# Layer norm with a tile of its own for the centred, weighted row: one step out of place instead of in place

## The chip, the cores and the metric

The kernel runs on one core of a Trainium2 chip. The metric is the device time of one execution in microseconds (us); the median of three executions of the kernel before is 1938.56 us (1937.89 to 1939.11). The core's engines run their own instruction streams in order and meet through semaphores: TensorE (PE in the profile, with PEld for its weight loads), VectorE (DVE), ScalarE (ACT), GpSimd (POOL) and SyncE (SP), which issues most DMAs.

## The reference

Two decoder layers over x of 512 tokens by 1024 channels in float32. Each layer is a half-step SwiGLU FFN, a token mixer (layer 0: differential attention; layer 1: causal pooling), cross-attention into 256 memory tokens, and a second FFN. Every one of these eight sublayers ends in a layer norm over the 1024 channels of the residual sum:

```python
def layer_norm(x, g, b):
    xf = x.astype(jnp.float32)
    mu = jnp.mean(xf, axis=-1, keepdims=True)
    var = jnp.mean(jnp.square(xf - mu), axis=-1, keepdims=True)
    y = (xf - mu) * lax.rsqrt(var + LN_EPS) * g.astype(jnp.float32) + b.astype(jnp.float32)
    return y.astype(x.dtype)
...
    for i in range(DEPTH):
        x = layer_norm(a * x + 0.5 * swiglu_ffn(x, ffn_w_in[i, 0], ffn_w_out[i, 0]), ln_g[i, 0], ln_b[i, 0])
        ...  # h = diff_attention(x, ...) in layer 0, pool_mixer(x, ...) in layer 1
        x = layer_norm(a * x + h, ln_g[i, 1], ln_b[i, 1])
        x = layer_norm(a * x + memory_cross_attention(x, mem, xa_wq[i], xa_wkv[i], xa_wo[i]), ln_g[i, 2], ln_b[i, 2])
        x = layer_norm(a * x + 0.5 * swiglu_ffn(x, ffn_w_in[i, 1], ffn_w_out[i, 1]), ln_g[i, 3], ln_b[i, 3])
```

## The kernel before

The 512 tokens are four tiles X[0] to X[3] of 128 tokens by 1024 channels, kept in SBUF as float32 for the whole run. Every product is made of three matmuls of split operands: a value is split into a high part (ScalarE's cast, L114) and a low part (VectorE's subtraction, L115), and `mm3` (L201 to L203) runs high by high, high by low and low by high. So nearly everything that TensorE reads, weights (wh, wl) and activations (xh, xl), passes through ScalarE and VectorE first.

A sublayer's last product gives 128x512 blocks `ps` in PSUM, in the order LAST: (half, token tile) = (0,0), (0,1), (1,0), (1,1), (0,2), (1,2), (0,3), (1,3). `ln_add` (L397, VectorE) adds each block into X and collects its row sums. When the second half of a token tile is in, `ln_token` runs for it; there are 8 norms of 4 token tiles, 32 in all. Its steps:

- L406, VectorE: the (negative) mean from the two row sums.
- L419, ScalarE ("square"): Square of X plus the mean, summed along the row into `var`. The squares themselves go to a throw-away bfloat16 tile `sq`, taken from the buffers of the tag `self.spare`: sp in the FFNs, rt in differential attention, p in cross-attention, sq in the pooling mixer.
- L420 and L421, GpSimd: variance times 1/D plus epsilon, and its power -0.5, both on 128x1 values.
- L423, VectorE ("begin"): (X plus mean) times g, written to y. In the kernel before y is X itself, so this write comes after ScalarE's read of X. The one exception is the last token tile of the last norm, where y is two tiles of the tag sp.
- L425, VectorE ("end"): y times the power of L421 plus b, written to X.

The gain g and the shift b are loaded by DMA into tiles of the phase's tags (`self.gain`): hr and sr in the FFNs, v and v in differential attention, gb and gb in cross-attention, pooled and pooled in the pooling mixer (there as two halves each, and begin and end go in two 128x512 instructions; so they do in the last norm).

After end, TensorE transposes X (L479, `turn`) into `pt`, and ScalarE and VectorE split the transposes into xh and xl, the next sublayer's operands. `turn_late` puts these transposes behind given matmuls (`issue_after`), so their place in TensorE's stream is set by hand. `split_weights` puts some weight splits behind a norm's square and end (gates, L241 and L243). `queue_behind` in `ffn` puts the last token tile's square and begin behind the first weight split of the next FFN.

The order within each engine's stream comes from a planner that takes instructions by their place in the program and by its own estimate of when their inputs are ready, and that gives a tile a buffer of its tag when one has been released. A buffer is released when all instructions that use the tile are done. Each phase (FFN, mixer, cross-attention) opens its own pools over the same memory, so that a buffer of the next phase waits for the tile that had the place before.

In cross-attention, `xa_head` holds the softmax rows of two token tiles in one p tile (128x2x256), two such tiles for a head, out of 4 buffers; `turn_memory` loads the 256 memory tokens into 4 tiles of the same tag before the first head.

Of the kernel before, what the change touches and what calls it, by code (L numbers as in the profile page):

```python
# [17 lines left out]
P = 128  # L18
D = 1024
S = 512  # L20
# [5 lines left out]
MEM = 256  # L26
# [73 lines left out]
def drain(units):  # L100
    for _ in units:
        pass


class Trunk:
# [40 lines left out]
        self.pad(ctx, APART)  # L146

    @contextmanager
    def phase_pool(self, gain, spare, **bufs):

        self.gain, self.spare, self.bufs, self.phase = gain, spare, bufs, {}
        with ExitStack() as ctx:
            for t in bufs:
                if t == "_x":
                    self.to_x(ctx)
                else:
                    self.phase[t] = ctx.enter_context(self.pool(t))
            yield  # L160
# [240 lines left out]
    def ln_token(self, t):  # L401
        nc, X = self.nc, self.X[t]
        g, b = self.ln_gb
        s = self.ln_sums[t]
        mean, var, rstd = (self.small(n, (P, 1)) for n in ("mean", "var", "rstd"))
        nc.vector.tensor_scalar(mean, s[:, 0:1], s[:, 1:2], -1.0 / D, ALU.add, ALU.mult)  # L406
        if self.last_ln or not self.wide_gain:
            cols = [slice(half * S, (half + 1) * S) for half in range(2)]
        else:
            cols = [slice(0, D)]  # L410
        if self.wide_gain:
            g, b = ([x[0][:, c] for c in cols] for x in (g, b))
        y = [X[:, c] for c in cols]
        if self.last_ln and t == NT - 1:
            y = [self.tmp(self.spare) for _ in range(2)]
            sq = self.act(self.gain[0], (P, D), mybir.dt.bfloat16)
        else:
            sq = self.act(self.spare, (P, D), mybir.dt.bfloat16)
        square = nc.scalar.activation(sq, X, AF.Square, bias=mean, accum_out=var)  # L419
        nc.gpsimd.tensor_scalar(var, var, 1.0 / D, EPS * self.ln_scale**2, ALU.mult, ALU.add)  # L420
        nc.gpsimd.tensor_tensor(rstd, var, self.mhalf[:, 0:1], ALU.pow)  # L421
        for i, c in enumerate(cols):
            begin = nc.vector.scalar_tensor_tensor(y[i], X[:, c], mean, g[i], ALU.add, ALU.mult)  # L423
        for i, c in enumerate(cols):
            end = nc.vector.scalar_tensor_tensor(X[:, c], y[i], rstd, b[i], ALU.mult, ALU.add)  # L425
            if self.last_ln:
                nc.sync.dma_start(self.out[t * P : (t + 1) * P, c], X[:, c])
        self.ends.append((square, end))
        self.begins = square, begin
        if t == NT - 1:  # L430
            self.gates = list(self.next_gates)
        if self.make_xt:
            self.late.append(t)
# [794 lines left out]
    def turn_memory(self, tag):  # L1228

        nc = self.nc  # L1230
        src = self.a["mem"][0].rearrange("(m p) (h d) -> p m h d", p=P, h=2)
        raw = [[self.tmp(tag) for h in range(2)] for m in range(2)]
        for m in range(2):
            for h in range(2):
                nc.sync.dma_start(raw[m][h], src[:, m, h])
        self.memT = []
        for c in range(0, KC, 2):
            pt = self.aux("pt").rearrange("p (c m n) -> p c m n", c=2, m=2)
            for i in range(2):
                for m in range(2):  # L1240
                    o = (c + i) % 4 * P
                    self.nc.tensor.transpose(pt[:, i, m], raw[m][c // 4][:, o : o + P], self.ident)
            t = self.mem_tile(c)
            self.split(t[:, 0], t[:, 1], pt.rearrange("p c m n -> p c (m n)"))
        self.stage["mem"].tile([P, (480 - LINE) // 4], F32, name="mempad")
# [47 lines left out]
    def xa_head(self, qs, kt, v):  # L1293
        nc = self.nc
        pT = [self.pair("pT") for _ in range(2)]
        ps = []
        for tt in range(0, NT, 2):
            sc = self.aux("xs").rearrange("p (t n) -> p t n", t=2)
            for i in range(2):
                o = slice((tt + i) * P, (tt + i + 1) * P)  # L1300
                for c in range(2):
                    q = qs[c]
                    self.mm3(
                        sc[:, i], (q[0][:, o], q[1][:, o]), (kt[0][:, c], kt[1][:, c]), c == 0, c == 1
                    )
            mx, sm, rc = self.small("mx"), self.small("sm"), self.small("rx")
            nc.vector.tensor_reduce(mx, sc, AX.X, ALU.max, negate=True)
            p = self.tmp("p", (P, 2, MEM))
            for i in range(2):
                nc.scalar.activation(  # L1310
                    p[:, i], sc[:, i], AF.Exp, bias=mx[:, i : i + 1], accum_out=sm[:, i : i + 1]
                )
            nc.vector.reciprocal(rc, sm)
            for i in range(2):
                nc.vector.tensor_scalar(p[:, i], p[:, i], rc[:, i : i + 1], None, ALU.mult)
            ps.append(p)
            yield
        for tt in range(0, NT, 2):
            p = ps[tt // 2]
            pt = self.aux("pt").rearrange("p (m i n) -> p m i n", m=2, i=2)  # L1320
            for m in range(2):
                for i in range(2):
                    nc.tensor.transpose(pt[:, m, i], p[:, i, m * P : (m + 1) * P], self.ident)
            for m in range(2):
                o = slice(tt * P, (tt + 2) * P)
                self.split(pT[m][0][:, o], pT[m][1][:, o], pt[:, m].rearrange("p i n -> p (i n)"))
            yield
        for c in range(2):
            e = slice(c * P, (c + 1) * P)
            po = self.aux("xo")  # L1330
            for m in range(2):
                self.mm3(po, (v[0][:, m, e], v[1][:, m, e]), pT[m], m == 0, m == 1)
            o = self.pair("oT")
            self.split(o[0], o[1], po)
            self.oT.append(o)
            yield
# [45 lines left out]
    def cross_attention(self, layer, ln):  # L1382
        bufs = dict(q=8, oT=10, gb=2)
        if layer == 0:
            self.kv = []
            mem = self.side_pool("mem")
            with self.other_pools():
                self.stage["mem"] = mem
                with self.phase_pool(("gb", "gb"), "p", pT=6, p=4, kv=8, _x=0, **bufs):
                    self.kvp = self.phase["kv"]  # L1390
                    self.mem_tiles = []
                    with self.tc.high_priority():
                        self.turn_memory("p")
                    self.xa(layer, ln)
            self.close_side()
        else:
            with self.later, self.phase_pool(("gb", "gb"), "p", pT=6, p=4, **bufs):
                self.xa(layer, ln)

    def xa(self, layer, ln):  # L1400
# [58 lines left out]

    def ffn_phase(self, **more):  # L1460
        bufs = dict(b1=1, b3=1, b2=1, b4=1, _x=0, xe=6, hb=4, sp=4, ha=4, sr=1, hr=3)
        return self.phase_pool(("hr", "sr"), "sp", **bufs, **more)

    def ffn_first(self, layer, ln):
        with self.ffn_pools():
# [13 lines left out]
    def mixer(self, layer, ln):  # L1479
        if layer == 0:  # L1480
            bufs = dict(low=4, rt=2, a=4, p=4, o=1, qk=8, _x=0, v=4, oT=11, mask=1)
            with self.other_pools(), self.phase_pool(("v", "v"), "rt", **bufs):
                self.diff_attention(layer, ln)
            self.close_side()
        else:
            w = self.a["xa_wkv"][layer]
            self.later = ExitStack()
            self.later.enter_context(self.late_pools())
            self.kvp = self.later.enter_context(self.pool("kv"))
            with self.phase_pool(("pooled", "pooled"), "sq", pooled=20, sq=1):  # L1490
                with self.tc.high_priority():
                    keys = self.load_cols(w, 0, "rawe")
                    self.load_memory()
                    ahead = [self.halves(t, "we", "we") for t in keys]
                    self.pool_weights()
                    self.raw_order = ["rawe", "raw", "raw"]
                side = self.pool_mixer(layer, ln)
                next(side)
                self.kv = []
                self.weave(self.first_heads(layer, ahead), side, 900, 6000)  # L1500
                drain(self.early_kv(layer, (1,), self.ahead))
            self.close_side()
# [40 lines left out]
```

## Time and profile before

| what | value |
|---|---|
| median of three executions | 1938.56 us (1937.89 to 1939.11) |
| profiled execution: its own time, its span | 1939.3 us, 1937.5 us |
| granted TensorE clock | 0.999 |
| PE busy | 1904.6 us (98%) |
| DVE busy | 1555.8 us (80%) |
| ACT busy | 1015.8 us (52%) |
| POOL busy | 334.8 us (17%) |

The span runs from the first to the last instruction; 1.8 us of the profiled execution's own time lie around it. A row of the timeline gives the start and the duration in us, then engine, line, operation, names (out<-in) and shapes, and in brackets the idle time of the engine before it and what ended that. Rows of equal instructions right behind each other are merged (x2, x4). A row of the waits gives the total, the number and the longest. Engine queues have a q (SPq issues DMAs). A line can be a helper's: L114 and L115 are all splits.

### The profile page before, as it was taken

The page shows a single profiled execution, that of the slowest core. Times are in us where ns is not written, and L with a number is a line of the kernel's source. Part 1 is how long each engine was busy: PE and PEld are TensorE (multiplying, and loading weights), DVE is VectorE, ACT ScalarE, POOL GpSimd, SP SyncE. Part 2 cuts the span into 40 slices and gives each one's busy share as a digit, 9 for nine tenths or more (in the row PEclk, how much of TensorE's full clock was granted, in tenths as well). Part 3 has the DMA queues.
Part 4 walks back from the last instruction along what each step waited for, and adds up shares of the span by engine and source line. Part 5 has one row for each costly group of instructions (what it writes and reads, how often), then busy time and mean ns, then how long its engine had stood idle before and what let it go on. Part 6 is the DMA issues. An engine that isn't in the chain of part 4 may idle for free.

```text
span 1937.5 us, 32405 instructions
## 1 busy us (share of the span) xinstructions
PE 1904.6 (98%) x12988; PEld 1738.8 (90%) x12988; DVE 1555.8 (80%) x2262; ACT 1015.8 (52%) x1543; POOL 334.8 (17%) x318
## 2 busy tenths in 40 slices
PE   9999999999999999999999999999999999999998
PEld 8999998888888888999998999999898889999996
DVE  7988887888867558788888988898886568898886
ACT  6655553567755435645554655455454436555552
POOL 2212121111211002211220321212110013211211
PEclk9999999999999999999999999999999999999999
DMA  9878772322126326978784688877444337777861
GB/s 253 198 173 185 171 145 66 92 67 87 56 97 196 109 66 153 218 175 163 141 193 135 114 203 174 178 161 164 142 153 141 109 87 122 190 174 168 187 140 44
DMA packets 254199, 280.46 MB, mean 145 GB/s; under 512 B 9184, under 2 KB 221792, under 8 KB 254048
## 3 DMA queue, kind: packets, MB, share of 16 engines
q0 software_dynamic: 95808, 102.77, 32.6%
q1 hardware_dynamic: 158240, 175.61, 28.6%
q8 instruction: 102, 1.67, 0.3%
q14 instruction: 49, 0.40, 0.1%
HBM read 274.15 MB, written 4.20 MB: 144 GB/s over the span
## 4 chain that ended last, share of the span: by engine, by line
PE 70%; DVE 17%; ACT 4%; DMA 4%; issue 2%; POOL 2%; SPq 0%; DVEq 0%; POOLq 0%; ACTq 0%
PE x L202 6%; PE x L201 6%; PE x L203 6%; PE z L202 4%; PE z L201 4%; PE z L203 4%; DVE wl L115 4%; PE ps L203 3%; PE ps L202 3%; DMA ra<-in_ffn_w_in_dram 3%; PE ps L201 3%; PE px L201 2%; PE px L203 2%; PE px L202 2%; PE xq L202 2%
## 5 line engine op out<-in xcount | busy, mean ns | idle before, releaser
L636 POOL DMA_DIRECT2D ra<-in_ffn_w_in_dram x132 | 170.4, 1315 | 988.3 <-DVE wl L115 971.4
L114 ACT CAST wh<-ra 128x1024 fp32r<-128x1024 f32 x184 | 193.3, 1053 | 209.1 <-PE x L202 56.0
L115 DVE TENSOR_TENSOR wl<-ra,wh 128x1024 fp32r<-128x1024 f32 x184 | 224.0, 1223 | 68.0 <-ACT wh L114 67.2
L114 ACT CAST wh<-rc 128x1024 fp32r<-128x1024 f32 x136 | 142.8, 1052 | 117.7 <-PE x L202 42.5
L201 PE MATMUL x<-xe,wh 128*128 128x256 f32 x704 | 195.6, 278 | 1.6 <-ACT sp L697 1.6
L201 PE MATMUL x<-xh,wh 128*128 128x256 f32 x704 | 196.0, 278 | 0.7 <-ACT xh L114 0.7
L202 PE MATMUL x<-xl,wh 128*128 128x256 f32 x704 | 195.6, 278 | 0.3 <-DVE xl L115 0.3
L203 PE MATMUL x<-xh,wl 128*128 128x256 f32 x704 | 195.6, 278 | 0.4 <-DVE wl L115 0.4
L202 PE MATMUL x<-xe,wh 128*128 128x256 f32 x704 | 195.3, 277 | 0.0
L203 PE MATMUL x<-xe,wl 128*128 128x256 f32 x704 | 195.3, 277 | 0.0
L114 ACT CAST wh<-b 128x1024 fp32r<-128x1024 f32 x112 | 117.8, 1051 | 128.6 <-PE x L202 63.2
L115 DVE TENSOR_TENSOR wl<-rc,wh 128x1024 fp32r<-128x1024 f32 x136 | 164.9, 1222 | 23.2 <-ACT wh L114 23.2
L115 DVE TENSOR_TENSOR wl<-b,wh 128x1024 fp32r<-128x1024 f32 x112 | 137.0, 1224 | 41.1 <-ACT wh L114 41.1
L201 PEld LDWEIGHTS x<-xe,wh 128*128 128x128 f32 x704 | 132.5, 188 | 3.2 <-ACT sp L697 1.8
L202 PEld LDWEIGHTS x<-xl,wh 128*128 128x128 f32 x704 | 132.7, 188 | 2.1 <-DVE xl L115 0.8
L201 PEld LDWEIGHTS x<-xh,wh 128*128 128x128 f32 x704 | 132.3, 188 | 2.2 <-ACT xh L114 0.9
L202 PEld LDWEIGHTS x<-xe,wh 128*128 128x128 f32 x704 | 132.5, 188 | 1.4
L203 PEld LDWEIGHTS x<-xh,wl 128*128 128x128 f32 x704 | 132.3, 188 | 0.6 <-DVE wl L115 0.6
L203 PEld LDWEIGHTS x<-xe,wl 128*128 128x128 f32 x704 | 132.4, 188 | 0.0
L203 PE MATMUL y<-xh,wl 128*128 128x256 f32 x352 | 98.8, 281 | 2.1 <-DVE wl L115 1.2
L201 PE MATMUL y<-xh,wh 128*128 128x256 f32 x352 | 98.1, 279 | 0.2 <-ACT wh L114 0.2
L202 PE MATMUL z<-xe,wh 128*128 128x256 f32 x352 | 97.8, 278 | 0.3 <-DVE xe L115 0.3
(401 smaller groups left out, 6056.0 us busy)
## 6 DMA issues: line engine op xcount, KB each, us to landing
ra<-in_ffn_w_in_dram POOLq DMA_DIRECT2D x132, 512.0 KB, 6.9
rc<-in_ffn_w_in_dram SPq DMA_DIRECT2D x88, 512.0 KB, 6.1
b<-in_ffn_w_out_dram SPq DMA_DIRECT2D x60, 512.0 KB, 5.0
ra<-in_ffn_w_in_dram SPq DMA_DIRECT2D x44, 512.0 KB, 5.0
rc<-in_ffn_w_in_dram POOLq DMA_DIRECT2D x44, 512.0 KB, 7.2
b<-in_ffn_w_out_dram POOLq DMA_DIRECT2D x16, 512.0 KB, 12.6
raw<-in_da_w_qkv_dram SPq DMA_DIRECT2D x16, 512.0 KB, 5.1
raw<-in_xa_wkv_dram SPq DMA_DIRECT2D x8, 1024.0 KB, 5.5
```

The lines of the kernel that those rows point to most:

```text
L114: self.nc.scalar.copy(hi, src),
L115: self.nc.vector.tensor_sub(lo, src, hi.bitcast(F32)),
L201: mm(out, w[0], x[0], start=start, stop=False, skip_group_check=again)
L202: mm(out, w[0], x[1], start=False, stop=False, skip_group_check=again)
L203: self.last_mm = mm(out, w[1], x[0], start=False, stop=stop, skip_group_check=again)
L636: self.last_more = nc.gpsimd.dma_start(t, source(*block), accum_op=ALU.add)
```

## The change

Begin writes y to a tile of its own (`home`): a whole 128x1024 tile, or two 128x512 tiles in the pooling mixer. The tag of this tile is a new argument of `phase_pool`: hr in the FFNs, v in differential attention, p in cross-attention, pooled in the pooling mixer. The last token tile of the last norm stays as it was. To have buffers of 128x1024 under the tag p, `xa_head` and `turn_memory` take p tiles of double size, and p has 2 buffers in place of 4, so the same bytes; pooled has 22 buffers in place of 20; hr (3) and v (4) keep theirs.

```diff
     @contextmanager
-    def phase_pool(self, gain, spare, **bufs):
+    def phase_pool(self, gain, spare, home, **bufs):
-        self.gain, self.spare, self.bufs, self.phase = gain, spare, bufs, {}
+        self.gain, self.spare, self.home = gain, spare, home
+        self.bufs, self.phase = bufs, {}
...
         if self.wide_gain:
             g, b = ([x[0][:, c] for c in cols] for x in (g, b))
-        y = [X[:, c] for c in cols]
         if self.last_ln and t == NT - 1:
             y = [self.tmp(self.spare) for _ in range(2)]
             sq = self.act(self.gain[0], (P, D), mybir.dt.bfloat16)
         else:
             sq = self.act(self.spare, (P, D), mybir.dt.bfloat16)
+            if self.wide_gain:
+                whole = self.tmp(self.home, (P, D))
+                y = [whole[:, c] for c in cols]
+            else:
+                y = [self.tmp(self.home) for _ in cols]
...
     def turn_memory(self, tag):
-        raw = [[self.tmp(tag) for h in range(2)] for m in range(2)]
+        raw = [self.tmp(tag, (P, 2, S)) for m in range(2)]
         for m in range(2):
             for h in range(2):
-                nc.sync.dma_start(raw[m][h], src[:, m, h])
+                nc.sync.dma_start(raw[m][:, h], src[:, m, h])
...
-                    self.nc.tensor.transpose(pt[:, i, m], raw[m][c // 4][:, o : o + P], self.ident)
+                    self.nc.tensor.transpose(pt[:, i, m], raw[m][:, c // 4, o : o + P], self.ident)
...
     def xa_head(self, qs, kt, v):
-        ps = []
+        ps = self.tmp("p", (P, 2, 2, MEM))
         for tt in range(0, NT, 2):
...
-            p = self.tmp("p", (P, 2, MEM))
+            p = ps[:, tt // 2]
...
-            ps.append(p)
             yield
         for tt in range(0, NT, 2):
-            p = ps[tt // 2]
+            p = ps[:, tt // 2]
...
-                with self.phase_pool(("gb", "gb"), "p", pT=6, p=4, kv=8, _x=0, **bufs):
+                with self.phase_pool(("gb", "gb"), "p", "p", pT=6, p=2, kv=8, _x=0, **bufs):
...
-            with self.later, self.phase_pool(("gb", "gb"), "p", pT=6, p=4, **bufs):
+            with self.later, self.phase_pool(("gb", "gb"), "p", "p", pT=6, p=2, **bufs):
...
-        return self.phase_pool(("hr", "sr"), "sp", **bufs, **more)
+        return self.phase_pool(("hr", "sr"), "sp", "hr", **bufs, **more)
...
-            with self.other_pools(), self.phase_pool(("v", "v"), "rt", **bufs):
+            with self.other_pools(), self.phase_pool(("v", "v"), "rt", "v", **bufs):
...
-            with self.phase_pool(("pooled", "pooled"), "sq", pooled=20, sq=1):
+            with self.phase_pool(("pooled", "pooled"), "sq", "pooled", pooled=22, sq=1):
```

## The prediction

> **What bounds the kernel now.** I read the page first, then TensorE's waits, then a table of stretches, then the timeline around the norms.
>
> ```profile
> span 1937.5 us, 32405 instructions
> ...
> PE 1904.6 (98%) x12988; PEld 1738.8 (90%) x12988; DVE 1555.8 (80%) x2262; ACT 1015.8 (52%) x1543; POOL 334.8 (17%) x318
> ...
> PE 70%; DVE 17%; ACT 4%; DMA 4%; issue 2%; POOL 2%; SPq 0%; DVEq 0%; POOLq 0%; ACTq 0%
> ```
>
> TensorE's waits for the norm's end, for `ln_add`, and for VectorE where the memory is transposed:
>
> ```profile
> PE pt L479 <- DVE X L425: 4.2, 5, 2.5
> ```
>
> ```profile
> PE ps L201 <- DVE X L397: 1.3, 1, 1.3
> ```
>
> ```profile
> PE pt L1242 <- DVE xl L115: 1.2, 3, 0.5
> ```
>
> And the last stretch (length, then busy time of PE, PEld, DVE, ACT, POOL):
>
> ```profile
> 1929.70:1937.50 7.80, 0.00 (x0) 0.00 (x0) 3.59 (x7) 1.24 (x2) 0.73 (x2) 0.81 0.18 67
> ```
>
> TensorE is busy for 1904.6 of 1937.5 us, so 32.9 us are idle, and 7.8 us of those are the tail after its last matmul. A change to the norms can only be worth what TensorE waits for them. The three rows of waits say how little that is: 4.2 us in five waits of transposes (L479) for a norm's end (L425), one wait of 1.3 us for a PSUM buffer that `ln_add` (L397) frees late, and 1.2 us in three waits behind VectorE in the stage where the memory is transposed.
>
> **The norm's chain, before and after.** The first norm's last token tile, VectorE, then ScalarE, then GpSimd:
>
> ```profile
> 343.48 0.21 DVE L406 TENSOR_SCALAR mean<-sums 128x1 f32<-128x1 f32 x1
> 345.00 1.28 DVE L423 SCALAR_TENSOR_TENSOR X<-X,mean,hr 128x1024 f32<-128x1024 f32 x1 [1.31 <-ACT sp L419]
> ...
> 347.05 1.28 DVE L425 SCALAR_TENSOR_TENSOR X<-X,rstd,sr 128x1024 f32<-128x1024 f32 x1 [0.44 <-POOL rstd L421]
> ```
>
> ```profile
> 343.73 1.15 ACT L419 ACTIVATE sp<-X,mean 128x1024 bf16<-128x1024 f32 x1 [3.59 <-DVE mean L406]
> ```
>
> ```profile
> 345.06 1.28 POOL L420 TENSOR_SCALAR var<-var 128x1 f32<-128x1 f32 x1 [8.70 <-ACT sp L419]
> 346.42 0.59 POOL L421 TENSOR_TENSOR rstd<-var,mhalf 128x1 f32<-128x1 f32 x1
> ```
>
> Mean to end takes 347.05 - 343.48 = 3.57 us. VectorE idles 1.31 us until the square has read X. Then begin and GpSimd's L420 start together, and L420, a 128x1 instruction, takes as long as begin (1.28 us). The last norm's last token tile already has its y elsewhere:
>
> ```profile
> 1930.28 0.21 DVE L406 TENSOR_SCALAR mean<-sums 128x1 f32<-128x1 f32 x1
> 1930.53 1.41 DVE L423 SCALAR_TENSOR_TENSOR sp<-X,mean,hr 128x512 f32<-128x512 f32 x2
> 1930.61 1.15 ACT L419 ACTIVATE hr<-X,mean 128x1024 bf16<-128x1024 f32 x1 [7.02 <-DVE mean L406]
> ```
>
> ```profile
> 1931.94 0.19 POOL L420 TENSOR_SCALAR var<-var 128x1 f32<-128x1 f32 x1 [6.50 <-ACT hr L419]
> 1932.21 0.54 POOL L421 TENSOR_TENSOR rstd<-var,mhalf 128x1 f32<-128x1 f32 x1
> 1932.79 1.42 DVE L425 SCALAR_TENSOR_TENSOR X<-sp,rstd,sr 128x512 f32<-128x512 f32 x2 [0.84 <-POOL rstd L421]
> ```
>
> This is the changed form, measured: begin and square side by side at their usual length (the square 1.15 us in both), L420 in 0.19 us since begin is over, and mean to end 1932.79 - 1930.28 = 2.51 us. The change is worth 3.57 - 2.51 = 1.06 us of chain for a token tile where VectorE has nothing else to do. Part of it is the square, part is GpSimd no longer running beside begin.
>
> The Trainium skill, page "SBUF — State Buffer", section "Who interferes with whom", says that a VectorE instruction with two SBUF inputs and a GpSimd instruction that reads SBUF exclude each other for the whole instruction, and the later one waits. This trace agrees (1.28 us beside begin, 0.19 us alone). The rule also speaks against the change: any other such VectorE instruction behind begin holds GpSimd just as well, and if that happened at every token tile the sum below would fall to what the square alone gives, or less.
>
> **The change part by part.**
>
> Instructions: none is added or removed on any engine. 32 means, squares and pairs on GpSimd, and as many begins and ends, keep shape and length; writing to another tile costs nothing (1.41 us for two halves in the row above). VectorE is as busy as before; what changes is where it idles and the planner's order, since begin is ready right after the mean.
>
> The tail: the last token tile already has this form, and TensorE's end lies ahead of it. Worth 0.
>
> First norm, last token tile. TensorE's waits behind it, and what stands between:
>
> ```profile
> 348.39 1.09 PE L479 MATMUL pt<-ident,X 128*128 128x128 f32 x8 [0.19 <-DVE X L425]
> 350.22 0.38 PE L201 MATMUL v<-wh,xh 128*128 128x256 f32 x1 [0.74 <-ACT xh L114]
> 351.19 0.50 PE L201 MATMUL q<-xh,wh 128*128 128x512 f32 x1 [0.47 <-ACT xh L114]
> 352.31 0.39 PE L203 MATMUL v<-wh,xl 128*128 128x256 f32 x1 [0.62 <-DVE xl L115]
> ```
>
> ```profile
> 348.25 0.28 DVE L923 TENSOR_REDUCE lam_d<-p 128x2 f32<-128x128 f32 x1
> ```
>
> ```profile
> 348.20 1.28 ACT L924 ACT_TABLE_LOAD   x1
> 349.49 0.20 ACT L924 ACTIVATE lam_d<-lam_d 128x2 f32<-128x2 f32 x1
> 349.60 2.03 ACT L114 CAST xh<-pt 128x512 fp32r<-128x512 f32 x4
> ```
>
> The four waits are 0.19 + 0.74 + 0.47 + 0.62 = 2.02 us, all on one string: end, then L923 on VectorE, then L924 with its table on ScalarE, then the four casts xh, with VectorE's splits behind end as well. If the string starts 1.06 us earlier, TensorE gains that 1.06; the rest of the 2.02 stays. Bounds 0 (the planner puts another split ahead of end) and 2.02. I take 1.06.
>
> Norm of differential attention. Here three memory transposes wait behind VectorE; the first follows this:
>
> ```profile
> 580.79 1.28 DVE L425 SCALAR_TENSOR_TENSOR X<-X,rstd,v 128x1024 f32<-128x1024 f32 x1 [0.72 <-POOL rstd L421]
> ```
>
> ```profile
> 583.94 0.66 PE L1242 MATMUL pt<-ident,p 128*128 128x128 f32 x4 [0.53 <-DVE xl L115]
> ```
>
> End waited 0.72 us for GpSimd, and `ln_add` and the split xl stand behind it. With 1.06 us off, the 0.53 goes; what is late next are the two other memory transposes (1.2 - 0.53, about 0.6 us), behind VectorE's unbroken work. I take 0.53, between 0 and 1.2.
>
> Its last token tile is where GpSimd suffers most:
>
> ```profile
> 595.11 2.60 POOL L421 TENSOR_TENSOR rstd<-var,mhalf 128x1 f32<-128x1 f32 x1
> ```
>
> ```profile
> 599.18 1.06 PE L479 MATMUL pt<-ident,X 128*128 128x128 f32 x8 [0.62 <-DVE X L425]
> ```
>
> L421 takes 2.60 us against 0.54, a loss of 2.06 on the way to end, because VectorE runs weight splits and begin without a break. With begin earlier, a split still follows. TensorE's wait is 0.62; I take 0.40, between 0 and 0.62.
>
> Cross-attention of layer 0, first token tile:
>
> ```profile
> 741.12 1.23 DVE L115 TENSOR_TENSOR wl<-ra,wh 128x1024 fp32r<-128x1024 f32 x1 [0.84 <-ACT wh L114]
> 742.26 1.22 DVE L115 TENSOR_TENSOR wl<-rc,wh 128x1024 fp32r<-128x1024 f32 x1
> 743.40 1.28 DVE L423 SCALAR_TENSOR_TENSOR X<-X,mean,gb 128x1024 f32<-128x1024 f32 x1
> 744.59 0.68 DVE L397 SCALAR_TENSOR_TENSOR X<-X,ps 128x512 f32<-128x512 f32 x1
> ```
>
> Begin comes after two weight splits since its square is late, and `ln_add` behind it frees the PSUM buffer for which TensorE waits its 1.3 us. With begin ready at the mean, it fills the 0.84 us of idle time and the row of 744.59 comes 0.84 earlier. I take 0.84, between 0 and 1.3.
>
> The other waits of the group of 4.2: the longest, 2.54 us, is the pooling mixer's first token tile, whose begin waits for g itself:
>
> ```profile
> 1438.28 1.42 DVE L423 SCALAR_TENSOR_TENSOR X<-X,mean,pooled 128x512 f32<-128x512 f32 x2 [2.64 <-DMA pooled<-in_ln_g_dram]
> ```
>
> The change doesn't touch this load: 0. The two left are 4.2 - 2.54 - 0.19 - 0.62 = about 0.85 us in places where VectorE has no idle time; I take 0.20, between 0 and 0.85. The other norms' token tiles cost TensorE nothing now: their transposes stand far enough behind in its stream. If that cover went, the price is such a wait, at most the 1.3 us seen.
>
> Buffers. In cross-attention y and sq share the two p buffers: sq(t+1) takes the one that sq(t) left, y(t+1) the one that end(t) left, and end(t) is ahead of begin(t+1) on VectorE anyway: 0. A p tile of double size is released after the head's second half; heads run one after another, so the tile of two heads ago is free: 0. In hr and v the y's have free buffers beside the gains; pooled has two more. On SP, the four memory loads come in the same number and place; they are issued from 558.14 on:
>
> ```profile
> 558.14 2.69 SPq L1235 DMA_DIRECT2D p<-in_mem_dram  x4
> ```
>
> Their data are first read some 25 us later, at 583.94, so a wait for a larger buffer, even of some us, is hidden, and so is the weight load behind them on that queue. y keeps its buffer until end instead of until begin, so the next phase's tiles in that place may come some 1.3 us later; POOL's memset of `mask` and its SP load are such, and the scores that read them come tens of us later: 0, with a bound of 0.5 us of loss.
>
> Sum: 1.06 + 0.53 + 0.40 + 0.84 + 0.20 = 3.03 us. Against the profiled execution: span 1937.5 to 1934.5, own time 1939.3 (1.8 around the span) to 1936.3. That execution is 0.74 us above the median of the three, so the median goes from 1938.56 to 1935.5. What a measurement of this kernel tells from no change is about 0.2%, 3.9 us: the forecast lies inside it.
>
> **The rivals.**
>
> More goes. All the touched waits together are 2.02 + 1.2 + 0.62 + 1.3 + 0.85 = 6.0 us, so 1932.6. For it: VectorE's lost idle time (1.31 us before each such begin) also pulls ahead splits that later matmuls wait for. Against it: each string has a next link, as in the first norm, where only half goes. Past 3.9 us this counts as faster.
>
> Nothing comes of it: 1938.5, give or take 1. The planner, told that begin is ready, fills the idle time with begin and then leaves VectorE idle before end (0.84 us in the tail's row) with the same instructions behind it; TensorE's waits move and stay as long. Or y finds no free buffer and waits for the square after all, above all with p, which serves both. For it: only 6 us of 1937.5 are there to win.
>
> Slower: end stalls VectorE. The planner sets end early, believing GpSimd done, while a split holds GpSimd as at 595.11; `ln_add` behind end then frees PSUM late, at 1.3 us a time, the largest such wait seen. Six norms with transposes behind them, one such wait in each: 7.8 us less the 3.0 won, so 1943.3. It decides from three such waits on. Against it: today's end has the same GpSimd ahead of it at 32 places and only one wait of this kind is in the trace.
>
> **How the numbers follow.** Forecast (a gain of 1 to 3.9 us): 0.37. More goes: 0.34. Nothing comes of it: 0.15. Slower than by 0.2%: 0.14. So faster 0.34, within 0.2% 0.52, slower 0.14. The range goes from the whole of the touched waits (1932.6) to a part of the slower case, one or two new waits beyond the gain, 1940.9; about 0.08 is left out below and 0.11 above. The forecast's own range is 1934.7 to 1937.6.
>
> **What would show it.** Right: L423 no longer idles for L419 and starts within 0.1 us of the mean's end; L420 falls from 1.28 us towards 0.2; mean to end nears 2.5 us; the one wait of L201 on L397 shrinks from 1.3 to some 0.4; the four waits near 350 sum to about 1; the 2.5 us of the pooling mixer and the 7.8 us tail stay. Wrong: new TensorE waits on L397 or L425; L421 at 2 us and more in many places; VectorE's order changed so that a split which TensorE needs comes behind a begin; or a changed SP order that moves the loads of g, in which case the 2.54 us would move by as much either way.

## The result and the profile after

Side by side on one chip, 14 runs each, the changed kernel has a median of 1936.1 us (1933.4 to 1939.6) and the kernel before 1938.6 us (1936.5 to 1941.6): ratio 0.9984 [0.9977, 0.9991], that is 1.7 to 4.5 us less. A second comparison, beside the experiments, gave 0.9986 [0.9978, 0.9995]. The forecast was 1935.5 us.

The page of the profiled execution after (its own time 1937.6 us):

```profile
span 1935.8 us, 32409 instructions
...
PE 1906.2 (98%) x12988; PEld 1743.4 (90%) x12988; DVE 1556.6 (80%) x2262; ACT 1016.7 (53%) x1543; POOL 308.5 (16%) x318
```

TensorE idles 1935.8 - 1906.2 = 29.6 us instead of 32.9, 3.3 us less; its busy time is 1.6 us longer, for the most part because 3.41 us near 1438 us ran at half clock (shown below), so the span is only 1.7 us shorter. VectorE is as busy as before; GpSimd has lost 26 us. The groups of begin and of GpSimd's two steps say why, first in the kernel before, then in the changed one (count, busy us, mean ns, then idle time before them and its releaser; lines have moved: L397 is now L398, L419 to L421 are L424 to L426, L423 is L428, L425 is L430, L479 is L484, L201 to L203 are L202 to L204):

```profile
L423 DVE SCALAR_TENSOR_TENSOR X<-X,mean,hr 128x1024 f32<-128x1024 f32 (+1 forms) x18 | 19.7, 1106 | 15.2 <-ACT sp L419 15.2
...
L420 POOL TENSOR_SCALAR var<-var 128x1 f32<-128x1 f32 x32 | 31.1, 973 | 264.4 <-ACT sp L419 169.9 <-ACT sq L419 37.5 <-ACT p L419 25.3
L421 POOL TENSOR_TENSOR rstd<-var,mhalf 128x1 f32<-128x1 f32 x32 | 24.1, 752 | 2.7
```

```profile
L428 DVE SCALAR_TENSOR_TENSOR hr<-X,mean,hr 128x1024 f32<-128x1024 f32 (+1 forms) x18 | 19.7, 1106 | 0.4
...
L426 POOL TENSOR_TENSOR rstd<-var,mhalf 128x1 f32<-128x1 f32 x32 | 19.2, 598 | 2.7
L425 POOL TENSOR_SCALAR var<-var 128x1 f32<-128x1 f32 x32 | 10.2, 318 | 282.8 <-ACT sp L424 179.8 <-ACT sq L424 32.1 <-ACT rt L424 29.3
```

Begin of the FFNs' norms idled 15.2 us for the square and now idles 0.4; GpSimd's first step falls from a mean of 973 ns to 318, which is 20.9 of the 26 us. The first norm's last token tile, on VectorE, ScalarE and GpSimd:

```profile
344.08 0.21 DVE L407 TENSOR_SCALAR mean<-sums 128x1 f32<-128x1 f32 x1
344.32 1.28 DVE L428 SCALAR_TENSOR_TENSOR hr<-X,mean,hr 128x1024 f32<-128x1024 f32 x1
346.51 1.28 DVE L430 SCALAR_TENSOR_TENSOR X<-hr,rstd,sr 128x1024 f32<-128x1024 f32 x1 [0.90 <-POOL rstd L426]
```

```profile
344.32 1.15 ACT L424 ACTIVATE sp<-X,mean 128x1024 bf16<-128x1024 f32 x1 [3.02 <-DVE mean L407]
```

```profile
345.65 0.19 POOL L425 TENSOR_SCALAR var<-var 128x1 f32<-128x1 f32 x1 [9.23 <-ACT sp L424]
345.93 0.55 POOL L426 TENSOR_TENSOR rstd<-var,mhalf 128x1 f32<-128x1 f32 x1
```

Begin and square start in the same 10 ns; mean to end is 346.51 - 344.08 = 2.43 us instead of 3.57. Of the four waits of TensorE behind it (2.02 us) one is left:

```profile
351.51 0.39 PE L204 MATMUL v<-wh,xl 128*128 128x256 f32 x1 [0.93 <-DVE xl L115]
```

The waits that answer to the prediction's groups, from the table of TensorE's waits after (total, times, longest):

```profile
PE pt L484 <- DVE X L430: 4.9, 3, 2.7
...
PE x L203 <- DVE xl L115: 1.5, 1, 1.5
...
PE pt L1247 <- DVE xl L115: 0.7, 1, 0.7
```

The wait for `ln_add` (1.3 us) has gone, the memory's transposes wait 0.7 instead of 1.2 us, the transposes of X wait 4.9 instead of 4.2 us, and a wait of 1.5 us for a split xl is new.

Where the time went, stage by stage, is read from the start times of equally numbered matmuls. The table gives the us between two such starts in the traces of the two kernels and of a second run of each (both described below):

| matmuls (us in the trace before) | before | again | after | again | mean difference |
|---|---|---|---|---|---|
| 2450-2550, first norm (348-367) | 19.59 | 21.01 | 17.86 | 17.85 | -2.44 |
| 3750-3950, norm of diff. attention (580-613) | 32.77 | 33.78 | 33.13 | 33.36 | -0.03 |
| 4700-4800, cross-attention, layer 0 (737-758) | 20.47 | 20.11 | 20.65 | 21.08 | +0.57 |
| 7200-8200, first FFN of layer 1 (1091-1220) | 129.11 | 130.31 | 128.36 | 128.36 | -1.35 |
| 9700-9900, pooling mixer (1436-1467) | 30.83 | 29.88 | 32.77 | 32.45 | +2.26 |
| 10750-11300, last FFN (1615-1683) | 68.19 | 68.57 | 67.68 | 67.71 | -0.68 |

The six sum to -1.7 us; the spans of the four traces differ by 1.95 us in the mean. Stages ahead of the first touched norm differ by about 1 us between traces too, so only lines that repeat carry weight. Three gains stand against two losses that the prediction had as 0 and as a gain. The second and third line don't stand clear of chance: the kernel of the first experiment below, in which begin is in place, took 32.07 and 21.37 us there.

### The profile page after: what moved, and what is told of

It is laid out like the page before. It is cut to its first block, busy times and chain, and to the rows that moved or that the text cites. A ratio compares the mean times of both kernels' runs of the same rounds, so it can differ in the third digit from the quotient of the medians.

```text
span 1935.8 us, 32409 instructions
## 1 busy us (share of the span) xinstructions
PE 1906.2 (98%) x12988; PEld 1743.4 (90%) x12988; DVE 1556.6 (80%) x2262; ACT 1016.7 (53%) x1543; POOL 308.5 (16%) x318
## 4 chain that ended last, share of the span: by engine, by line
PE 75%; DVE 14%; DMA 4%; ACT 4%; issue 2%; POOL 1%; SPq 0%; DVEq 0%; POOLq 0%; ACTq 0%
PE x L202 6%; PE x L203 6%; PE x L204 6%; PE ps L204 4%; PE ps L203 4%; PE ps L202 4%; PE z L202 4%; PE z L204 4%; PE z L203 4%; DVE wl L115 3%; DMA ra<-in_ffn_w_in_dram 2%; PE px L202 2%; PE px L204 2%; PE px L203 2%; PE y L204 2%
## 5 line engine op out<-in xcount | busy, mean ns | idle before, releaser
L202 PE MATMUL x<-xh,wh 128*128 128x256 f32 x704 | 196.9, 280 | 1.4 <-ACT xh L114 1.4
L203 PE MATMUL x<-xl,wh 128*128 128x256 f32 x704 | 196.6, 279 | 1.5 <-DVE xl L115 1.5
L204 PE MATMUL x<-xh,wl 128*128 128x256 f32 x704 | 196.3, 279 | 0.0
L202 PE MATMUL x<-xe,wh 128*128 128x256 f32 x704 | 195.7, 278 | 0.4 <-ACT sp L702 0.4
L203 PE MATMUL x<-xe,wh 128*128 128x256 f32 x704 | 195.5, 278 | 0.0
L204 PE MATMUL x<-xe,wl 128*128 128x256 f32 x704 | 195.4, 278 | 0.0
L203 PEld LDWEIGHTS x<-xl,wh 128*128 128x128 f32 x704 | 133.6, 190 | 3.3 <-DVE xl L115 2.0
L202 PEld LDWEIGHTS x<-xh,wh 128*128 128x128 f32 x704 | 132.9, 189 | 2.9 <-ACT xh L114 1.6
L202 PEld LDWEIGHTS x<-xe,wh 128*128 128x128 f32 x704 | 132.3, 188 | 1.9 <-ACT sp L702 0.6
L203 PEld LDWEIGHTS x<-xe,wh 128*128 128x128 f32 x704 | 132.7, 188 | 1.3
L204 PEld LDWEIGHTS x<-xh,wl 128*128 128x128 f32 x704 | 133.2, 189 | 0.0
L204 PEld LDWEIGHTS x<-xe,wl 128*128 128x128 f32 x704 | 132.5, 188 | 0.0
L204 PE MATMUL y<-xh,wl 128*128 128x256 f32 x352 | 98.7, 280 | 0.9
L202 PE MATMUL y<-xh,wh 128*128 128x256 f32 x352 | 98.2, 279 | 0.4 <-ACT wh L114 0.4
L202 PE MATMUL z<-xe,wh 128*128 128x256 f32 x352 | 97.9, 278 | 0.0
```

The lines of the kernel that those rows point to most:

```text
L202: mm(out, w[0], x[0], start=start, stop=False, skip_group_check=again)
L203: mm(out, w[0], x[1], start=False, stop=False, skip_group_check=again)
L204: self.last_mm = mm(out, w[1], x[0], start=False, stop=stop, skip_group_check=again)
```

## The experiments

All ratios are to the kernel before, run beside them.

**The new buffers alone, begin in place.** First question: does the gain come from begin's freedom, or from the buffers and the order that they bring?

```diff
-                y = [self.tmp(self.home) for _ in cols]   # and the whole tile
+        y = [X[:, c] for c in cols]
```

> The changed kernel's buffers (p 2 of double size, pooled 22), but y is X again: begin is in place. Theory A (the gain is the shorter way from mean to end, because begin no longer waits for the square): time as before, 1938.6 within its noise of about 1.5 us; begin idles about 1.3 us for the square; GpSimd's first step takes 1.28 us beside begin; TensorE's waits near 350 us sum to about 2.0 and the 1.25 us wait for ln_add near 745 us is back. Theory B (the gain comes from the buffers and the order that they give): time as the changed kernel, 1936.1, with the waits near 350 at about 0.9.

1940.6 us, ratio 0.9995 [0.9986, 1.0005]: no gain. TensorE's four waits near 350 us sum to 2.27 us, and it waits for `ln_add` again (1.00 and 1.07 us at 741 and 748 us). Begin idles for the square again (the group's row from this kernel):

```profile
L424 DVE SCALAR_TENSOR_TENSOR X<-X,mean,hr 128x1024 f32<-128x1024 f32 (+1 forms) x18 | 19.7, 1106 | 15.3 <-ACT sp L420 15.3
```

**The whole change, with the wait put back.** Begin writes to its own tile and waits for the square all the same.

```diff
+            if not (self.last_ln and t == NT - 1):
+                self.tc.add_manual_dep(begin.ins, square.ins.name, ...)
```

> The changed kernel with tiles of their own for y, but begin is made to wait for the square by a semaphore (28 of 32 token tiles wait as in the kernel before; the last of the last norm doesn't). Theory A: 1938.6 within 1.5 us, mean to end of the first norm's last token tile back at 3.5 us (2.43 in the changed kernel), GpSimd's first step 1.28 us beside begin. Theory B: 1936.1, since tiles and buffers are those of the changed kernel.

1939.8 us, 1.0001 [0.9991, 1.001]. The first norm, VectorE and TensorE (the end is L433 here):

```profile
347.07 1.28 DVE L428 SCALAR_TENSOR_TENSOR hr<-X,mean,hr 128x1024 f32<-128x1024 f32 x1 [1.31 <-ACT sp L424]
```

```profile
350.41 1.09 PE L487 MATMUL pt<-ident,X 128*128 128x128 f32 x8 [0.15 <-DVE X L433]
352.44 0.39 PE L202 MATMUL v<-wh,xh 128*128 128x256 f32 x1 [0.94 <-ACT xh L114]
353.42 0.50 PE L202 MATMUL q<-xh,wh 128*128 128x512 f32 x1 [0.47 <-ACT xh L114]
354.34 0.58 PE L204 MATMUL v<-wh,xl 128*128 128x256 f32 x1 [0.42 <-DVE xl L115]
```

Begin waits at 31 token tiles here, all but the last of the last norm (not at 28, as expected). The 1.31 us and the four waits (0.15 + 0.94 + 0.47 + 0.42 = 1.98 us) are back, mean to end is 3.52 us, and the whole time is back with them. So the gain comes from begin's freedom; theory B, the buffers and the order that they give, falls. What belongs to the shorter chain itself and what to the new order of VectorE that begin's freedom allows is not separated by this.

**Both kernels once more.**

> The changed kernel again, for a second trace and for the noise of single waits. Theory A: 1936.1 within 1.5 us, ratio 0.998 to 0.9991; the waits near 350 us sum to about 0.9 again, those near 745 stay away, and those near 598 (1.44 us) and 754 (1.54 us) come again if they belong to the order of the instructions. If they were chance (a late weight load), one or both are gone. Theory B says nothing else on this run.

> The kernel before again, for a second trace. Both theories: ratio 1.000 within 0.001. The waits of the first trace that belong to the order come again at 348 to 352 (2.0 us in four) and at 745 (1.25 us); those that are chance differ, which bounds what one trace can say of a stage (my guess from the stretch ahead of the first norm, where both programs are the same and the traces differ by 1.2 us: about 1 us a stage).

The changed kernel 0.9986 [0.9978, 0.9995], the kernel before 1.0003 [0.9994, 1.0012]. In the second trace of the changed kernel the waits near 598 and 754 us come again (1.86 and 1.54 us, after 1.44 and 1.54), so they belong to its order. In the second trace of the kernel before the wait for `ln_add` comes again (1.06 us), and the 0.62 us near 599 us does not. The second trace of the kernel before shows something that the first had not: a spell of half clock. The same 17 us behind the first norm, first and second trace (length, busy PE, PEld, DVE, ACT, POOL, granted clock, DMA share, GB/s):

```profile
340.00:357.00 17.00, 14.97 (x114) 13.71 (x113) 12.28 (x23) 7.61 (x13) 2.24 (x3) 1.00 0.45 136
```

```profile
340.00:357.00 17.00, 15.02 (x102) 13.71 (x101) 12.47 (x23) 7.48 (x12) 2.20 (x3) 0.90 0.44 135
```

17 x (1 - 0.90) = 1.7 us are lost there; the clock record of the trace has 0.5 for 3.41 us. The two kernels in the experiments above have it too (0.90 and 0.91), the changed kernel in neither trace, nor do the seven later traces in which begin is free at this norm.

**Is the clock part of the gain?** In the kernel before, eight transposes that nobody reads are put into TensorE's stream at the first norm, to fill its idle time there.

```diff
+        pf = self.aux("fill")                    # behind the norm's transposes
+        with self.behind(): transpose4(pf, [ident] * 4)   # twice
```

> The kernel before, with eight 128x128 transposes of the identity into an unused PSUM tile right behind the transposes of the first norm's last token tile. They add about 0.8 us of TensorE work where TensorE waits 0.74 to 0.94 us for xh, and nothing else changes. Open is why the kernel before is 1.4 us slower near 357 us in three of four traces than in the first: in those three the granted clock is 0.5 for 3.41 us from 352 to 354 us on, in none of the changed kernel's two. Theory A1 (the waits near 350 us make the clock drop, and this is part of what the change saves): TensorE has less idle time there, so no drop to 0.5 near 352 us, and about 1.7 us less than the kernel before in executions that had one: ratio 0.9992 to 0.9997. Theory A2 (only the waits count, the clock is chance): ratio 1.000 within 0.0005, a drop near 352 us as often as before.

1939.7 us, 1.0003 [0.9993, 1.0013]. The clock stays at 1.00 in that stretch of its trace, yet the time is no better. The run doesn't decide between the theories, though: TensorE's waits there are 0.69, 0.27 and 0.96 us, 1.93 in sum, hardly less than the 1.98 to 2.27 without the transposes, so the idle time was moved rather than filled. A share of the clock in the gain is not shown; by the runs' mean clocks it is small: 0.9974 in the 11 runs of the changed kernel, 0.9974 in the 12 of the kernel before. The spell near 353 us has gone, but both traces of the changed kernel have one near 1438 us that neither trace of the kernel before has.

**The late wait of differential attention.** In the changed kernel the last token tile's transposes wait 1.44 us where 0.62 were before. TensorE, VectorE and ScalarE there:

```profile
598.28 1.06 PE L484 MATMUL pt<-ident,X 128*128 128x128 f32 x8 [1.44 <-DVE X L430]
```

```profile
592.93 1.28 DVE L428 SCALAR_TENSOR_TENSOR v<-X,mean,v 128x1024 f32<-128x1024 f32 x1
595.72 1.22 DVE L115 TENSOR_TENSOR wl<-raw,wh 128x1024 fp32r<-128x1024 f32 x1 [1.51 <-ACT wh L114]
596.86 1.28 DVE L430 SCALAR_TENSOR_TENSOR X<-v,rstd 128x1024 f32<-128x1024 f32 x1
```

```profile
594.63 2.00 ACT L114 CAST wh<-raw 128x1024 fp32r<-128x1024 f32 x2 [1.42 <-DMA raw<-in_xa_wq_dram]
```

Begin has moved ahead; behind it the planner has put a weight split whose cast waits for its DMA, and end stands behind that split. The experiment puts the split behind end.

```diff
+        if self.ln_next == "xa" and layer == 0:
+            self.next_gates = (1, 2, 2, 2, 3, 3)
```

> The changed kernel, with the weight splits after the norm of differential attention put behind the norm's end, by gates. In both traces of the changed kernel VectorE comes to the last token tile's end only after a split that waits for a late weight load (1.51 us), and TensorE waits 1.44 and 1.86 us near 598 us. Theory A (order: an in-order engine stands at the split): that wait falls under 0.5 us, the time by 1 to 1.5 us against the changed kernel, ratio about 0.998. Rival (GpSimd held back by splits, as in the kernel before with 2.60 us): the wait stays over 1 us and L421's step takes over 1.5 us.

1934.8 us, 0.9977 [0.9966, 0.9988]. End (L432 here) is ahead of the split, and TensorE's wait falls to 0.63:

```profile
595.88 1.28 DVE L432 SCALAR_TENSOR_TENSOR X<-v,rstd 128x1024 f32<-128x1024 f32 x1 [0.71 <-POOL rstd L428]
597.08 1.22 DVE L244 TENSOR_TENSOR wl<-raw,wh 128x1024 fp32r<-128x1024 f32 x1
```

```profile
597.31 1.06 PE L486 MATMUL pt<-ident,X 128*128 128x128 f32 x8 [0.63 <-DVE X L432]
```

GpSimd's L428 takes 0.54 us, so the rival falls. The wait is no better than the 0.62 in the first trace of the kernel before, and above the 0.5 expected: the order explains the loss, and no gain was to be had at this wait. That the kernel as a whole came down by more than this one wait is within what two such intervals leave open.

**The gain g of the pooling mixer.** In the changed kernel begin there waits for the load of g, as before, and TensorE for the end:

```profile
1434.46 0.75 DVE L428 SCALAR_TENSOR_TENSOR pooled<-X,mean,pooled 128x512 f32<-128x512 f32 x1 [3.15 <-DMA pooled<-in_ln_g_dram]
```

```profile
1437.20 0.65 PE L484 MATMUL pt<-ident,X 128*128 128x128 f32 x4 [2.68 <-DVE X L430]
```

And 12 us from that wait on, with the granted clock behind the busy times:

```profile
1434.00:1446.00 12.00, 9.32 (x67) 9.03 (x66) 10.01 (x23) 4.03 (x7) 1.09 (x2) 0.86 0.20 76
```

The clock is 0.86 over 12 us: another 1.7 us. Neither the long wait nor the spell needs begin's freedom: with the wait for the square put back, TensorE waits 2.83 us here and the clock is 0.87. TensorE's wait differs from trace to trace (1.35 to 2.99 us in the ten traces that load g this late). The experiment loads g and b when the mixer begins, and the norm then uses these tiles.

```diff
+        self.wide_gain = False
+        self.early_gb = [self.load_row("pooled", self.a[n][layer, ln]) for n in ("ln_g", "ln_b")]
```

> The changed kernel, with the pooling mixer's g and b loaded at the start of the mixer instead of just before its norm. They move five places ahead in SP's queue. Theory A: begin of the first token tile no longer waits for the load (3.15 us), TensorE's 2.3 to 2.7 us wait near 1438 us falls to under 0.7, and the drop of the clock to 0.5 there (in both traces of the changed kernel) goes with it, another 1.7 us: 3 to 4 us less than the changed kernel, ratio 0.9965 to 0.998. Rival (the loads move ahead of weight loads that are needed as much): the same wait turns up at the pk and pv products, ratio 0.998 to 0.999.

1933.8 us, 0.9974 [0.9965, 0.9983]. TensorE's waits for the first and the second token tile, and the same stretch, in this kernel:

```profile
1433.78 0.65 PE L487 MATMUL pt<-ident,X 128*128 128x128 f32 x4 [0.21 <-DVE X L433]
...
1439.35 0.66 PE L487 MATMUL pt<-ident,X 128*128 128x128 f32 x4 [0.66 <-DVE X L433]
```

```profile
1434.00:1446.00 12.00, 10.86 (x91) 10.46 (x89) 10.48 (x23) 7.66 (x11) 2.15 (x4) 1.00 0.01 2
```

The wait of 2.68 us is 0.21 now; the next token tiles wait 0.66, 0.51 and 0.60 us instead. The rival's wait at the pv product didn't grow (0.62 us, 0.77 in the changed kernel). The interval still overlaps that of the changed kernel, and this trace has a spell of half clock elsewhere, behind a wait of 2.02 us near 597 us.

**Both edits.**

> The changed kernel with both of these edits (splits behind end, g and b early). Theory A: the gains add, 4 to 5.5 us less than the changed kernel, ratio 0.996 to 0.9975. Rival: where TensorE is busy for 98% of the span, each wait taken away is found again at the next link, ratio 0.998 or more.

> The kernel with both edits (gain early, split behind end) again, six runs of it being few: 0.9969 expected, 1932.7 us beside a kernel before of 1939, and no spell of half clock at 598 or 1438 us in its trace, since its waits there are 0.6 to 0.7 us.

1932.7 us, 0.9969 [0.9957, 0.998], and in a second comparison 1932.8 us, 0.9957 [0.9944, 0.997]. This beats the kernel before in both comparisons. That it beats the changed kernel too (0.9986 [0.9978, 0.9995]) is clear of the intervals in the second comparison only; in the first they just overlap. Its traces have no half clock behind 598 or 1438 us; one has a spell at 59 us.

**The pace of TensorE.** The table of stages shows a gain of 1.35 us in the first FFN of layer 1, where only a wait of 0.2 us had gone. Counting matmuls in 40 us of it, kernel before and changed kernel:

```profile
1100.00:1140.00 40.00, 40.00 (x342) 40.00 (x341) 32.38 (x34) 23.11 (x28) 13.13 (x13) 1.00 1.12 243
```

```profile
1100.00:1140.00 40.00, 40.00 (x355) 40.00 (x354) 31.07 (x33) 23.10 (x28) 13.34 (x13) 1.00 1.15 252
```

No idle time and full clock in both, the same matmuls, and 355 instead of 342. Two experiments put the wait back in one norm each: that before this FFN, and that before the last FFN, where the paces stand the other way round.

```diff
+            if self.norm == (0, 3):        # and in the second (1, 2)
+                self.tc.add_manual_dep(begin.ins, square.ins.name, ...)
```

> The changed kernel with begin waiting for the square again in one norm only, that behind the second FFN of layer 0 (near 1093 us). Theory P (pace): TensorE runs the 128x256 matmuls of a whole FFN at one of two paces, and which one is set by how it comes out of the norm before. From 1100 to 1140 us all five traces with the wait have 342 matmuls at clock 1.00 and all five without it 355, so some 500 matmuls cost 0.1178 instead of 0.1133 us, 2.2 us. P expects 342 there again, TensorE's wait of about 0.2 us at the norm's end back, and a time some 1.5 to 2.5 us above the changed kernel (ratio to before 0.9985 plus about 0.001, so near 0.9995). Rival Q: the pace comes from the order or the places of everything ahead, not from this norm: 355 stay, and the ratio stays at 0.9985 to 0.9987 (0.2 us of wait is all).

```profile
1100.00:1140.00 40.00, 40.00 (x342) 40.00 (x341) 32.38 (x35) 23.33 (x28) 13.87 (x13) 1.00 1.11 237
```

342 again, as P had it. One product x there, 264 matmuls from 1120 us on, takes 31.1 us in the kernel before and 29.9 in the changed one: 0.118 and 0.113 us each, from start to start (the windows also count matmuls that only reach into them). All six traces with the wait at this norm have the slow pace, all eight without it the fast one, so it is set at this norm and not by what lies ahead or by the tiles' places: TensorE, ScalarE and GpSimd run the same order in this kernel and the changed one, and VectorE's order differs in nine places between 1067 and 1093 us. The time, 1938.2 us and 0.9989 [0.998, 0.9998], lies between what P and Q gave, and the interval holds both.

A wait is not the only thing that sets the pace, though. In the second half of this FFN the two traces of the kernel before, the same program, run at different paces, and TensorE has no wait of even 0.1 us there in either:

```profile
1156.00:1210.00 54.00, 54.00 (x400) 50.89 (x399) 46.92 (x60) 28.95 (x35) 10.31 (x8) 1.00 0.77 164
1156.00:1210.00 54.00, 54.00 (x392) 50.92 (x391) 45.81 (x58) 27.46 (x34) 10.31 (x8) 1.00 0.78 168
```

From matmul 7800 to 8200 they take 55.6 and 56.6 us, most of the 1.2 us by which these two traces differ in the table of stages.

> The changed kernel with begin waiting for the square again in the norm behind cross-attention of layer 1 alone (near 1600 us). There the paces stand the other way: from 1616 to 1626 us all five traces with the wait have 91 matmuls, all five without it 87 or 88. P expects 91 again and TensorE's waits of about 0.3 us near 1602 and 1629 back; some 450 matmuls at 0.1133 for 0.1178 us are 2.0 us less, minus 0.6 for the waits and up to 1 us for weight splits that come late near 1670: between 1.5 us faster and 0.5 us slower than the changed kernel, ratio 0.9977 to 0.9988. Q: 88 stay and the time rises by 0.3 to 0.6 us (0.9987 to 0.9989).

The changed kernel, then this one, in the last FFN, and what TensorE waits for soon after in this one:

```profile
1616.00:1626.00 10.00, 10.00 (x88) 10.00 (x87) 9.96 (x12) 9.32 (x12) 3.17 (x3) 1.00 0.76 110
```

```profile
1616.00:1626.00 10.00, 10.00 (x90) 9.97 (x88) 10.00 (x11) 8.78 (x12) 4.07 (x4) 1.00 0.81 122
```

```profile
1669.46 0.38 PE L204 MATMUL y<-xh,wl 128*128 128x256 f32 x1 [1.01 <-DVE wl L115]
```

The pace changes as P said (90 matmuls), but the time is 1938.8 us, 0.9993 [0.9984, 1.0002], not 0.9977 to 0.9988. TensorE comes to the weights sooner and waits for their split; from matmul 10750 to 11300 this kernel takes 68.6 us and the changed one 67.7.

> The changed kernel with the pooling mixer's gain loaded early and the layer-0 query weight split behind end (as in the fastest kernel so far, 0.9969 [0.9957, 0.998]), and begin waiting for the square in the norm behind cross-attention of layer 1. P expects 91 matmuls from 1616 to 1626 us and 0 to 1.5 us less than the same kernel without that wait, measured beside it; Q expects 88 and 0.3 to 0.6 us more.

1934.0 us, 0.9969 [0.9957, 0.9981], against 1932.8 us of the same kernel without the wait: no gain here either. The window has 86 matmuls in 9.70 busy us, not 91, because a wait of 0.30 us falls into it; from one start to the next they take 0.113 us, so the pace is P's. TensorE then waits 0.89 us for a weight split at 1666 us. Here the faster pace bought nothing, since TensorE soon waited for its weights.

## Why the prediction was right, point by point

The sum forecast 3.03 us; the ratio makes it 3.1 (1.7 to 4.5), and the medians differ by 2.5. That begin's freedom is the cause is shown: with only the wait put back, all of the gain goes. The shorter chain is as forecast too. But that the sum came so close is luck. TensorE's own waits, term by term as below, make 1.09 + 0.16 - 0.82 - 0.29 + 0.09 = 0.23 us of the 3.03; the rest came from things that the sum didn't have.

- First norm, 1.06: right. Mean to end is 2.43 us (2.51 forecast), TensorE's four waits of 2.02 became one of 0.93, 1.09 less. The stage as a whole gave 2.4 us in the mean, half of a spell of 1.7 us included; without the spell it gave 1.5 to 1.7. A stop costs more than its idle time: in the kernel before, the matmul behind the 0.74 us starts 1.01 us after the one ahead of it, where 0.11 is usual. For the three stops that went, 0.4 to 0.6 us came on top of their waits.
- Norm of differential attention, 0.53: mis-sized. The three waits for VectorE of 0.53 + 0.48 + 0.16 became 0.67 and 0.34: 0.16 us less. The step had it the wrong way round: the 0.53 that was to go stayed, as 0.67, and the two others went, with a new wait of 0.34 us. End comes earlier, but a weight split (578.83 us, 1.22 us long) now stands between it and `ln_add`.
- Its last token tile, 0.40: wrong in sign, 0.62 became 1.44 (1.86 in the second trace; the second trace of the kernel before has no wait here). The step took VectorE's order as given once begin was earlier ("a split still follows" begin, it said, and named GpSimd as the sufferer). GpSimd was through in time; it was end that fell behind a split waiting for its DMA.
- Cross-attention of layer 0, 0.84: the wait for `ln_add`, 1.25 in the timeline, went altogether, though not because begin fills the idle time: VectorE still idles 0.67 us ahead of a split, and begin now comes behind one split instead of two. TensorE then ran into a new wait:

```profile
754.29 0.38 PE L203 MATMUL x<-xl,wh 128*128 128x256 f32 x1 [1.54 <-DVE xl L115]
```

```profile
752.35 1.29 DVE L430 SCALAR_TENSOR_TENSOR X<-p,rstd,gb 128x1024 f32<-128x1024 f32 x1 [0.37 <-POOL rstd L426]
753.55 1.28 DVE L115 TENSOR_TENSOR xl<-pt,xh 128x512 fp32r<-128x512 f32 x2
```

  The next token tile's begin and end stand ahead of the splits xl of this one. Net 0.3 us lost by the waits, 0.6 by the stage (not clear of chance, see the table). The prediction named this under what would make it wrong (a split that TensorE needs behind a begin), and did not price it. This cause is read from the trace (the wait, 1.52 to 1.54 us, is in all nine traces in which begin is free here); no experiment moved it.
- The pooling mixer, 0: the wait stayed (2.54, then 2.68), as said, but the stage lost 2.3 us: a new wait of 0.77 us for a split of weights and, in both traces of the changed kernel, the spell of half clock behind the long wait. The long wait and the spell came in the trace with the wait put back as well (32.62 us for the stage), so they can't be put down to begin's freedom alone.
- The tail, 0: right, 8.0 us from TensorE's end to the last instruction in both (the stretch of 7.8 us began 0.2 us behind that end). The places called others, 0.20: of the two waits for an end, 0.18 at 1094 us went and 0.69 at 1460 became 0.78, so 0.09; two waits for splits that the sum didn't list (0.35 at 1602 and 0.28 at 1629) went as well, and a new one of 0.52 came at 1156.
- Not in the sum at all: the pace of TensorE, about 2 us won in the first half of one FFN, and lost again in part in its second half. In the last FFN the changed kernel has the slower pace, but waits less for weights, and its stage is 0.7 us shorter.

The rival that more goes (faster by over 0.2%) isn't excluded by the interval, but the median, 1936.1 us, is 0.6 us from the forecast. The slower rival needed three new waits of 1.3 us; two came (1.44 and 1.54), of another kind than it named.

## What to carry to other kernels

When a step is freed from a wait, ask what the order puts into the place: here begin's freedom let a weight split slip ahead of end, and a begin and end ahead of a neighbour's splits, each a new wait of about 1.5 us; the first was mended by two lines of gates. A long wait just off the changed path (here for g's load, 1.35 to 2.99 us from trace to trace) can be worth as much as the change itself: loading g early gave 0.9974 beside 0.9986 for the change alone, with intervals that overlap, and with the other edit 0.9969 and 0.9957. A sum that comes out right is no proof of its terms; only the waits, read one by one, showed which had come. And when a 2 ms kernel moves by 3 us, compare stages between two traces of each kernel, since single traces differ by 1 to 2 us a stage.

## What the runs showed of the hardware

After TensorE has waited, the granted clock can drop to 0.5 for 3.41 us, a loss of 1.7 us: with single waits of 2.2 to 3.0 us near 1438 us (once for 6.83 us), of 2.0 us at 597 us and of 1.9 us at 59 us, and with four waits that sum to some 2 us within about 4 us at 350 us. It is so in some executions and not in others: waits of 2.54 us at 1440 us and of 2.99 us at 59 us left the clock at 1. The Trainium skill, page "TensorE: Matmul & The Clock Gate", section "What's actually happening", describes a free-running activity window of 3413 ns and half rate after about one idle window. The length agrees (3.41 us in the clock record); the idle time that brought it on here was shorter than a window. Over the 86 runs of the kernel before beside the experiments, mean clocks of 0.995 go with a mean of 1943.0 us (4 runs) and of 0.999 with 1937.1 us (7 runs), so this goes with a part of the spread of a single kernel's runs.

TensorE runs the same unbroken stream of 128x256 matmuls at one of two paces, 31.1 us / 264 = 0.118 us or 29.9 us / 264 = 0.113 us each, at full granted clock, for 50 us and more at a time. At one norm a wait of 0.2 us went with the slow pace in six traces of six, and its absence with the fast one in eight of eight. Elsewhere two executions of one program took different paces with no wait in the 55 us ahead. What in the engine makes the difference isn't shown.

A GpSimd instruction on 128x1 took 1.28 us beside begin and 0.19 us alone. That was in the trace before; over 32 token tiles it came to 20.9 us of GpSimd's busy time for this step, and with the wait put back the step's mean is 972 ns again.
